# A two-layer hybrid decoder step whose vector, scalar and queue order is set by a scheduler: the scheduler's machine model is exchanged

## The chip, the core and the metric

One core of a Trainium2 chip runs the whole kernel. The metric is the device time of one execution in microseconds; smaller is better. A core has engines with an instruction stream each: PE (TensorE: matmuls, with a loader of its own for the stationary operand, PEld in the profile), DVE (VectorE), ACT (ScalarE), POOL (GpSimd) and SP, which here only issues transfers. An engine runs its stream in order, and an instruction that has to wait for another engine or for a transfer holds back all that stands behind it on the same engine.

## The reference, cut to what matters

512 columns of a prompt and 8 x 4 of a sample group pass through two layers that share all weights (model width 1024, all in float32):

```
h = rmsnorm(x) * (1 + scale1(c)) + shift1(c);   z = h @ W_in
A: causal pooling      B: retention, 4 heads (normed per head, swish gate)
C: short gated conv    D: RWKV-7 time mixing (delta-rule state)
mixed = sum over A..D of sigmoid(gate_n of z) * (branch_n @ W_br_n)
x = x + gate1(c) * (mixed @ W_out)
h2 = rmsnorm(x) * (1 + scale2(c)) + shift2(c)
x = x + gate2(c) * (W_down(silu(a) * b)),   [a|b] = causal_dwconv3(h2 @ W_up)
```

A final rmsnorm follows, and the new states of all mixers are outputs too. The modulation (scales, shifts, gates) is a linear map of silu(c).

## The kernel before

**Tiles.** The 544 columns are handled in two halves of 272. Activations lie with the 1024 features on 128 partitions in 8 blocks. A weight unit is a tile of 128 x 1024, 138 units a layer. `load_unit` (L100 to L112) lets SP load it into `raw` (3 buffers), ACT cast it to a high part `whi` (L110) and DVE subtract to get the low part `wlo` (L111); `whi` and `wlo` have 4 buffers each. Only two units at the start have their subtraction on POOL. Activations are split the same way by `split_hilo`: a cast on ACT (L373), a subtraction on DVE (L374). A product is then three matmuls of 128 x 128 by 272 (`mm3`): high by high (L130), high by low part of the activation (L131), low part of the weight by high (L132). `unit` does this for eight blocks (24 matmuls) into one of three PSUM buffers called `pd`; five more, `pm`, serve the small matmuls.

**Pieces that the prediction speaks of.**
- The start (L890 to L932): x is loaded, its statistic made (L259, L262, L272, L286), the first modulation computed block by block (L196, copied to SBUF by ACT in L198, L201, DVE L203 and L185), x normalised (L926), modulated (L292 to L296) and split (L373, L374), while the first weight units are used block by block.
- RWKV (L377 onward): per pair of heads `p` an inverse norm, made by a sum over partitions (L362), a floor on DVE (L364), Ln on ACT (L365) and Exp on ACT (L370), for two column halves and two pairs. Then DVE forms the scan's operands: L414, L421, L422, and in `products()` L451, L453, L458 from two exponentials (L442, L443). The matmuls L477 and L484 use them. Each different ACT function may need another function table, which an ACT_TABLE_LOAD brings in.
- Then a triangular substitution on DVE: 31 steps of two instructions, L564 and L566, on data that comes back by a transfer (`in_xinit` among them, L537 to L539), and beside it four products L553 that read PSUM of L552. The scan over chunks follows (L583 to L673).
- Retention's norm: L362, then Ln (L367, straight from PSUM) and Exp (L370).
- The gates and branch projections (`gates`, about L1075 to L1117): for each of 8 blocks a `unit` with the gate's weights, whose PSUM goes through a sigmoid on ACT (L1108), and a projection of the branch (6 matmuls a half) whose PSUM is multiplied with it on DVE: L1091 in the first branch, L1093 in the others, which are then added by L1094 (POOL; DVE in the last branch). In the last branch the sum is split (L373, L374) as the operand of W_out, and `residual` (L342 to L348) adds the result to x.
- Short conv: L1022 to L1024, L1047, L1056 to L1065. FFN: L1238 to L1267. The last norm: L308 to L318.

**What sets the order.** The program is emitted in one pass. Small tasks are generators which `slot()` advances after a number of weight matmuls, so that their matmuls lie between the big ones:

```
with tile.TileContext(nc) as tc:
    with tc.manual_schedule(engines={mybir.EngineType.PE}):
        tile_hybrid_step(tc, io)
```

L1538 says that the PE keeps the order in which the program emits its matmuls. For DVE, ACT, POOL and SP the scheduler behind `TileContext` chooses: it plays the program through on a model of the machine and puts instructions in the order in which the model finds them ready. With the order come two other things. Which of a pool's buffers a new tile gets, and so whose end it has to wait for, depends on which tile the model finds free first. And ACT_TABLE_LOADs stand wherever the function on ACT changes in the final order.

## Time and profile before

| | |
|---|---|
| median of 3 runs | 1969.51 us (1968.21 to 1971.51) |
| profiled execution | 1970.54 us, its span 1968.8 us |
| mean granted clock of the PE | 0.997 |
| busy: PE, PEld, DVE, ACT, POOL | 98%, 93%, 53%, 41%, 16% of the span |
| moved | 227.23 MB, 115 GB/s on average |

A row of a timeline reads: start in us, duration in us, engine, line, operation, the tile written, the tiles read, the shape, and how many instructions it takes together; in brackets the idle time of the engine just before it and what ended that. Matmuls overlap: their durations (0.29 us) are longer than their step. The waits group such idle times by the pair of tiles: the line that waited, the line that released it, the total in us, how often, and the longest. Busy time of an engine other than the PE says little here, since it mostly lies beside the PE's.

### The profile page before, as it was taken

The numbers are of one execution on the slowest core, as the hardware profiler recorded it, in microseconds if no ns is written. First come the engines' busy times: TensorE is split into PE (matmuls) and PEld (weight loads), VectorE is DVE, ScalarE is ACT, GpSimd is POOL, SyncE is SP. The second block draws the span as 40 slices with busy tenths as digits, with TensorE's granted clock in tenths as the row PEclk, the third lists the DMA queues.
The fourth block names the chain that finished last, engine by engine and source line by source line (L and its number), as shares of the span: only waits on it lengthen the run. The fifth ranks groups of instructions, "written<-read, shape, count | busy, mean of one in ns | idle before, by whom it ended". The sixth has DMA issues, their size and how long they took to land.

```text
span 1968.8 us, 40136 instructions
## 1 busy us (share of the span) xinstructions
PE 1924.9 (98%) x16868; PEld 1834.8 (93%) x16868; DVE 1046.1 (53%) x2017; ACT 814.8 (41%) x1531; POOL 313.3 (16%) x589
## 2 busy tenths in 40 slices
PE   5999999999999999999999999999999999999997
PEld 5989888899998889999999998889999999999997
DVE  4476443543465444555664765345335665455565
ACT  4642322452355442435445423325423555243541
POOL 1110123213000110112202101241210022011210
PEclk9999999999999999999999999999999999999999
DMA  7324333433346742222332231134224132222221
GB/s 312 98 89 130 116 111 132 161 113 96 122 147 246 305 176 87 89 93 87 119 111 87 64 110 58 63 108 122 82 78 161 52 108 86 86 87 94 89 95 47
DMA packets 75557, 227.23 MB, mean 115 GB/s; under 512 B 20208, under 2 KB 23072, under 8 KB 73584
## 3 DMA queue, kind: packets, MB, share of 16 engines
q1 hardware_dynamic: 69872, 210.43, 32.2%
q0 software_dynamic: 3536, 11.53, 1.7%
q10 hardware_dynamic: 1968, 2.69, 0.5%
q8 instruction: 133, 2.18, 0.4%
q14 instruction: 48, 0.39, 0.1%
HBM read 213.33 MB, written 9.06 MB: 113 GB/s over the span
## 4 chain that ended last, share of the span: by engine, by line
PE 91%; DVE 4%; ACT 2%; DMA 2%; issue 1%; ACTq 0%; POOL 0%; DVEq 0%; POOLq 0%
PE pd L130 28%; PE pd L132 27%; PE pd L131 26%; PE pm L220 2%; DMA raw<-in_wst 1%; ACT whi L110 1%; DVE wlo L111 1%; PE pm L654 1%; PE pm L636 1%; PE pm L605 1%; DMA zr<-zr 1%; PE pm L658 1%; PE pm L593 0%; PE pm L477 0%; PE pm L484 0%
## 5 line engine op out<-in xcount | busy, mean ns | idle before, releaser
L130 PE MATMUL pd<-t,whi 128*128 128x272 f32 x4200 | 1234.8, 294 | 3.2 <-ACT t L373 1.8
L132 PE MATMUL pd<-t,wlo 128*128 128x272 f32 x4200 | 1214.5, 289 | 0.0
L131 PE MATMUL pd<-t,whi 128*128 128x272 f32 x4200 | 1208.5, 288 | 1.0 <-DVE t L374 0.8
L130 PEld LDWEIGHTS pd<-t,whi 128*128 128x128 f32 x4200 | 790.3, 188 | 41.4 <-issue 25.7
L131 PEld LDWEIGHTS pd<-t,whi 128*128 128x128 f32 x4200 | 792.5, 189 | 2.7 <-DVE t L374 1.8
L132 PEld LDWEIGHTS pd<-t,wlo 128*128 128x128 f32 x4200 | 791.3, 188 | 0.0
L111 DVE TENSOR_TENSOR wlo<-raw,whi 128x1024 fp32r<-128x1024 f32 x262 | 324.6, 1239 | 319.6 <-ACT whi L110 319.2
L110 ACT CAST whi<-raw 128x1024 fp32r<-128x1024 f32 x264 | 276.6, 1049 | 429.9 <-PE pd L131 417.3
L1256 POOL COPY off<-zr 128x18 f32<-128x18 f32 x88 | 77.2, 878 | 556.8 <-ACT zr L1254 556.8
L342 DVE SCALAR_TENSOR_TENSOR t<-pd,mod,t 128x272 f32<-128x272 f32 (+1 forms) x160 | 77.0, 482 | 106.9 <-PE pd L132 106.8
L1093 DVE TENSOR_TENSOR zr<-pd,zr 128x272 f32<-128x272 f32 x96 | 41.2, 438 | 124.9 <-PE pd L132 124.7
L1254 ACT COPY zr<-pd 128x272 f32<-128x272 f32 (+2 forms) x264 | 72.7, 311 | 72.9 <-PE pd L132 72.9
L1108 ACT ACTIVATE zr<-pd 128x272 f32<-128x272 f32 x128 | 50.5, 394 | 105.6 <-PE pd L132 105.5
L1094 POOL TENSOR_TENSOR t<-t,zr 128x272 f32<-128x272 f32 x64 | 68.9, 1093 | 119.5 <-DVE zr L1093 119.4
L1023 DVE SCALAR_TENSOR_TENSOR zr<-zr,par,zr 128x560 f32<-128x560 f32 x92 | 73.5, 801 | 9.7 <-ACT zr L1022 9.7
L1022 ACT ACTIVATE zr<-zr,par 128x560 f32<-128x560 f32 x92 | 70.2, 765 | 17.1 <-DVE zr L1047 9.6
L1024 DVE SCALAR_TENSOR_TENSOR zr<-zr,par,zr 128x560 f32<-128x560 f32 x92 | 73.4, 801 | 2.8
L373 ACT CAST t<-zr 128x544 fp32r<-128x544 f32 (+1 forms) x96 | 49.1, 530 | 61.8 <-DVE zr L1267 61.5
L374 DVE TENSOR_TENSOR t<-zr,t 128x544 fp32r<-128x544 f32 (+1 forms) x96 | 54.1, 580 | 30.0 <-ACT t L373 29.0
L259 ACT ACTIVATE zr<-t 128x272 f32<-128x272 f32 (+1 forms) x72 | 32.0, 454 | 86.6 <-DVE t L342 55.9
L610 DVE COPY z<-pm 32x128 f32<-32x128 f32 x34 | 9.8, 289 | 69.7 <-PE pm L605 69.4
L262 DVE TENSOR_TENSOR zr<-zr,zr 128x272 f32<-128x272 f32 (+1 forms) x63 | 29.9, 475 | 20.0 <-ACT zr L259 19.3
(286 smaller groups left out, 1635.1 us busy)
## 6 DMA issues: line engine op xcount, KB each, us to landing
raw<-in_wst SPq DMA_DIRECT2D x276, 512.0 KB, 3.5
t<-in_wada SPq DMA_DIRECT2D x32, 1024.0 KB, 9.7
raw<-in_wada SPq DMA_DIRECT2D x32, 512.0 KB, 3.6
zr<-in_rope POOLq DMA_DIRECT2D x16, 272.0 KB, 3.8
t<-in_xT SPq DMA_DIRECT2D x4, 544.0 KB, 6.7
zr<-zr ACTq DMA_DIRECT2D x32, 68.0 KB, 3.2
t<-in_xT SPq DMA_DIRECT2D x2, 1088.0 KB, 6.8
xs<-t SPq DMA_DIRECT2D x2, 1088.0 KB, 4.6
```

What stands on the lines that cost most here:

```text
L110: S.copy(hi, raw)
L111: (G if (l, u) in ((0, 1), (0, 2)) else V).tensor_tensor(out=lo, in0=raw, in1=hi, op=SUB)
L130: PE.matmul(ps, lhsT=a, rhs=xh, start=first, stop=False)
L131: PE.matmul(ps, lhsT=a, rhs=xl, start=False, stop=False)
L132: PE.matmul(ps, lhsT=b, rhs=xh, start=False, stop=last)
L342: V.scalar_tensor_tensor(out=x[:, c0:c0 + npc], in0=ps[:, :npc], scalar=gate[:, m, 0:1], in1=x[:, c0:c0 + npc], op0=MUL, op1=ADD)
L1022: S.activation(cv, u[:, 0:560], AF.Copy, scale=wcol(0))
L1023: V.scalar_tensor_tensor(out=cv, in0=u[:, 1:561], scalar=wcol(1), in1=cv, op0=MUL, op1=ADD)
L1024: V.scalar_tensor_tensor(out=cv, in0=u[:, 2:562], scalar=wcol(2), in1=cv, op0=MUL, op1=ADD)
L1094: (V if last else G).tensor_tensor(out=a[:, c0:c1], in0=a[:, c0:c1], in1=gs, op=ADD)
L1254: pad_evac(lambda o, i, sl: S.copy(o, i), u, ps, half, 2)
L1256: G.tensor_copy(off[:, 22 * s + j], u[:, 512:562].rearrange("p (x t) -> p x t", t=2)[:, 0:25:3, :])
```

## The change

One argument: the scheduler is to use the timeline simulator as its model of the machine, instead of the one that it has without it.

```diff
-    with tile.TileContext(nc) as tc:
+    with tile.TileContext(nc, schedule_with_timeline_sim=True) as tc:
         with tc.manual_schedule(engines={mybir.EngineType.PE}):
             tile_hybrid_step(tc, io)
```

The computation stays the same, instruction for instruction, and all rows of the PE stay where they are. DVE, ACT, POOL and SP get another order. The rows below group equal neighbours, so their counts differ: 1969 rows on DVE before and 1948 after, with 1208 lines of difference; 1523 and 1535 on ACT, with 653. ACT has six table loads more (42 instead of 36).

**ACT, RWKV's inverse norms in layer 0** (L365 is the Ln, L370 the Exp; `zr_143` belongs to the first pair of heads, `zr_146` to the second; L442 and L443 are the exponentials for the scan's operands). Before:

```order
L365 ACT_TABLE_LOAD
L365 ACTIVATE zr_143_1120<-zr_143_1120,eps_84 128x272 x2
L365 ACTIVATE zr_146_1129<-zr_146_1129,eps_84 128x272 x2
L370 ACT_TABLE_LOAD
L370 ACTIVATE zr_143_1120<-zr_143_1120 128x544
L370 ACTIVATE zr_146_1129<-zr_146_1129 128x544
L442 ACTIVATE zr_157_1179<-pm_156_1176 128x256
L443 ACTIVATE zr_157_1179<-pm_156_1176 128x256
```

After:

```order
L365 ACT_TABLE_LOAD
L365 ACTIVATE zr_143_1120<-zr_143_1120,eps_84 128x272 x2
L365 ACTIVATE zr_146_1129<-zr_146_1129,eps_84 128x272
L370 ACT_TABLE_LOAD
L370 ACTIVATE zr_143_1120<-zr_143_1120 128x544
L365 ACT_TABLE_LOAD
L365 ACTIVATE zr_146_1129<-zr_146_1129,eps_84 128x272
L370 ACT_TABLE_LOAD
L370 ACTIVATE zr_146_1129<-zr_146_1129 128x544
L442 ACTIVATE zr_157_1179<-pm_156_1176 128x256
L443 ACTIVATE zr_157_1179<-pm_156_1176 128x256
```

The last of the four Ln has moved behind the first Exp, and with it two table loads have come in. Layer 1 reads the same.

**DVE, the scan's operands at the same place** (L414 reads the Exp of ACT; L458 writes what the matmul L477 waits for; L1047 belongs to the short conv, L111 is the low part of a weight unit). Before:

```order
L422 TENSOR_TENSOR t4_75_624<-t4_75_624,zr_151_1159 128x544
L421 SCALAR_TENSOR_TENSOR t4_124_1008<-t4_124_1008 128x544
L422 TENSOR_TENSOR t4_75_624<-t4_75_624,zr_152_1163 128x544
L451 TENSOR_TENSOR t4_153_1173<-t4_124_1008,zr_157_1179 64x2x4x31
L453 TENSOR_TENSOR t4_153_1173<-t4_76_625,zr_157_1179 64x2x4x32
L451 TENSOR_TENSOR t4_154_1174<-t4_124_1008,zr_157_1179 64x2x4x31
L453 TENSOR_TENSOR t4_154_1174<-t4_76_625,zr_157_1179 64x2x4x32
L458 TENSOR_TENSOR zr_158_1189<-t4_124_1008,zr_157_1179 128x8x32
L458 TENSOR_TENSOR zr_158_1189<-t4_75_624,zr_157_1179 128x8x32
L1047 TENSOR_TENSOR zr_149_1145<-pd_150_1149,zr_128_1038 128x240
L1047 TENSOR_TENSOR zr_149_1145<-pd_150_1149,zr_128_1038 128x8x4
L111 TENSOR_TENSOR wlo_162_1211<-raw_160_1208,whi_161_1210 128x1024
```

After:

```order
L414 SCALAR_TENSOR_TENSOR t4_124_1008<-t4_75_624,nkk_67_608,zr_146_1129 128x544
L453 TENSOR_TENSOR t4_153_1173<-t4_76_625,zr_157_1179 64x2x4x32
L1047 TENSOR_TENSOR zr_149_1145<-pd_150_1149,zr_128_1038 128x240
L1047 TENSOR_TENSOR zr_149_1145<-pd_150_1149,zr_128_1038 128x8x4
L421 SCALAR_TENSOR_TENSOR t4_124_1008<-t4_124_1008 128x544
L422 TENSOR_TENSOR t4_75_624<-t4_75_624,zr_152_1163 128x544
L451 TENSOR_TENSOR t4_153_1173<-t4_124_1008,zr_157_1179 64x2x4x31
L451 TENSOR_TENSOR t4_154_1174<-t4_124_1008,zr_157_1179 64x2x4x31
L453 TENSOR_TENSOR t4_154_1174<-t4_76_625,zr_157_1179 64x2x4x32
L111 TENSOR_TENSOR wlo_162_1211<-raw_160_1208,whi_161_1210 128x1024
L458 TENSOR_TENSOR zr_158_1189<-t4_124_1008,zr_157_1179 128x8x32
L458 TENSOR_TENSOR zr_158_1189<-t4_75_624,zr_157_1179 128x8x32
```

L1047 and L111 have moved ahead of the two L458, and the second L414 (the first row here) behind the L421 and L422 of the first pair.

**DVE, the start of the substitution in layer 0** (L553 reads the PSUM of L552; the first L564 reads what the transfers bring; `t4_75` is the tile of the substitution). Before:

```order
L558 TENSOR_TENSOR sinv_63_604<-pm_232_1843,cst_82 32x64 x2
L553 TENSOR_TENSOR t4_124_1008<-pm_233_1848,t4_76_625 128x272
L553 TENSOR_TENSOR t4_124_1008<-pm_234_1851,t4_76_625 128x272
L553 TENSOR_TENSOR t4_124_1008<-pm_235_1854,t4_76_625 128x272
L553 TENSOR_TENSOR t4_124_1008<-pm_236_1857,t4_76_625 128x272
L564 TENSOR_TENSOR t4_75_624<-t4_75_624 128x31
L566 TENSOR_TENSOR t4_75_624<-t4_75_624 128x31
L564 TENSOR_TENSOR t4_75_624<-t4_75_624 128x30
```

After:

```order
L558 TENSOR_TENSOR sinv_63_604<-pm_232_1843,cst_82 32x64 x2
L564 TENSOR_TENSOR t4_75_624<-t4_75_624 128x31
L553 TENSOR_TENSOR t4_124_1008<-pm_233_1848,t4_76_625 128x272
L566 TENSOR_TENSOR t4_75_624<-t4_75_624 128x31
L553 TENSOR_TENSOR t4_124_1008<-pm_234_1851,t4_76_625 128x272
L564 TENSOR_TENSOR t4_75_624<-t4_75_624 128x30
L553 TENSOR_TENSOR t4_124_1008<-pm_235_1854,t4_76_625 128x272
L566 TENSOR_TENSOR t4_75_624<-t4_75_624 128x30
L553 TENSOR_TENSOR t4_124_1008<-pm_236_1857,t4_76_625 128x272
L564 TENSOR_TENSOR t4_75_624<-t4_75_624 128x2x29
L566 TENSOR_TENSOR t4_75_624<-t4_75_624 128x2x29
L564 TENSOR_TENSOR t4_75_624<-t4_75_624 128x2x28
```

The four L553 have moved from ahead of the first L564 to places between the substitution's first steps.

**Elsewhere, told in words.** Beside the norm of the second retention (about 432 us) ACT's order before is table load, L367, L367, table load, L1108, table load, L370; after, it is table load, L367, table load, L1108, table load, L367, table load, L370. Ahead of W_out (about 543 us) a pair of L374 stands right behind the last L1093 before; after, three L1094, another L374 and an L111 stand between them (in layer 1 two L111). In the start the copies L198 have moved ahead of weight casts (L110) and of the modulation (L292), and on SP the constants (L928 to L961) and two weight units have moved ahead of the last four pieces of the first modulation's weights (L898). Of the `pd` buffers, 37 gates begin in one whose last reader is an L1091 or L1093, where before it was a sigmoid L1108.

## The prediction

> **What bounds the kernel now.** I read the page's first part, then the waits of the PE alone, then windows and timelines where other engines hold the PE up.
>
> ```profile
> span 1968.8 us, 40136 instructions
> PE 1924.9 (98%) x16868; PEld 1834.8 (93%) x16868; DVE 1046.1 (53%) x2017; ACT 814.8 (41%) x1531; POOL 313.3 (16%) x589
> ```
>
> The PE works for 1924.9 of 1968.8 us, so 43.9 us are all that any order of the other engines could save. The PE's own order is written by hand and the change leaves every row of it alone. So the time changes only where an operand or a free PSUM buffer reaches the PE earlier or later than now. The waits of the PE (line that waits, who released it: us in total, times, longest):
>
> ```profile
> PE pm L272 <- DVE zr L262: 14.9, 2, 13.1
> PE pm L201 <- ACT t L198: 6.6, 2, 5.2
> PE pm L477 <- DVE zr L458: 2.8, 2, 1.4
> PE pm L636 <- DVE z L672: 1.6, 2, 0.8
> PE pd L130 <- DVE zr L346: 1.4, 1, 1.4
> PE pm L362 <- ACT zr L743: 1.2, 1, 1.2
> PE pd L130 <- DVE t L1192: 0.9, 1, 0.9
> PE pm L654 <- DVE z L610: 0.6, 2, 0.3
> ```
>
> The first row is the wait for the first loads (13.1 us) and one wait at the end; nothing there is reordered. Between them little is left to win. A stage without waits gives the price of one weight matmul (columns: window, its length, busy us and count of PE, PEld, DVE, ACT, POOL, clock, DMA share, GB/s):
>
> ```profile
> 800.00:930.00 130.00, 130.00 (x1037) 130.00 (x1037) 75.81 (x115) 60.30 (x109) 24.11 (x53) 1.00 0.28 90
> ```
>
> 130.00 / 1037 = 0.125 us each. The DVE is busy 58% of that window and ACT 46%: enough room for work to move freely, as long as nothing that the PE needs soon is put behind something slow. So I looked in the new order of DVE and ACT for places where a result needed within a few matmuls now stands behind other work. Four such places turned up, each once in each of the two layers.
>
> **First: the scan's operands (L458 to L477), 105 to 117 us.**
>
> ```profile
> 105.20 1.28 ACT L365 ACT_TABLE_LOAD   x1 [2.93 <-DVE zr L364]
> 106.50 1.76 ACT L365 ACTIVATE zr<-zr,eps 128x272 f32<-128x272 f32 x4
> 108.28 1.28 ACT L370 ACT_TABLE_LOAD   x1
> 109.57 1.21 ACT L370 ACTIVATE zr<-zr 128x544 f32<-128x544 f32 x2
> 110.27 1.48 DVE L414 SCALAR_TENSOR_TENSOR t<-t,nkk,zr 128x544 f32<-128x544 f32 x2 [2.58 <-ACT zr L370]
> 111.66 0.72 DVE L421 SCALAR_TENSOR_TENSOR t<-t 128x544 f32<-128x544 f32 x1
> 115.79 0.76 DVE L458 TENSOR_TENSOR zr<-t,zr 128x256 f32<-128x256 f32 x2
> 116.47 0.50 DVE L1047 TENSOR_TENSOR zr<-pd,zr 128x240 f32<-128x240 f32 x2
> 116.89 1.22 DVE L111 TENSOR_TENSOR wlo<-raw,whi 128x1024 fp32r<-128x1024 f32 x1
> 116.61 1.15 PE L477 MATMUL pm<-cst,zr 64*64 64x64 f32 x32 [1.39 <-DVE zr L458]
> ```
>
> Before: four Ln under one table, two Exp under another; the second Exp ends at 109.57 + 1.21 = 110.78. After: Ln, Ln, Ln, table, Exp, table, Ln, table, Exp: two more tables, so from 105.20 on 1.28 + 3 x 0.44 + 1.28 + 0.62 + 1.28 + 0.44 + 1.28 + 0.62, about 113.4. The second L414 waits for that, 2.6 us later. From 110.27 to 116.55 the DVE is dense: 6.28 us of L414 x2, L421 and L422 twice, L451 and L453 twice, L458 x2. After, the first L414, L421 and L422 (0.74 and twice 0.72, each less its overlap with its neighbour: 2.05 us) are done while ACT changes tables, but the two L1047 (0.4 without overlap) and L111 (1.15) have moved ahead of L458: 6.28 - 2.05 + 1.55 = 5.8, from 113.4 on, ends at 119.2 to 119.3. L477 starts about 2.7 to 2.8 us later; I take 2.8, the PE idle there 4.2 instead of 1.39. The waits' row (2.8 us in two) says that layer 1 has the same wait, and its order is the same: 2 x 2.8 = **+5.6**. Bounds: +4 if the DVE packs closer, +7 if L453 must also wait for the Exp behind it.
>
> After a table load the next ACTIVATE starts 0.02 us later (105.20 + 1.28, then 106.50). The Trainium skill ("ScalarE: Activation LUTs", section "What ACT_TABLE_LOAD costs") adds a drain of 1.38 us and has 2.66 us for every switch; by it the two switches would cost 5.3 us a layer and the term would be +11. The rows show no such drain, so the sum goes by 1.28.
>
> **Second: the gate after the substitution (L553, L564, L1091), 162 to 169 us.**
>
> ```profile
> 162.08 1.82 DVE L553 TENSOR_TENSOR t<-pm,t 128x272 f32<-128x272 f32 x4 [0.19 <-PE pm L552]
> 164.07 0.19 DVE L564 TENSOR_TENSOR t<-t 128x31 f32<-128x31 f32 x1 [0.17 <-DMA t<-in_xinit]
> 168.16 0.43 DVE L1091 TENSOR_TENSOR t<-pd,zr 128x272 f32<-128x272 f32 x1
> 168.53 0.37 PE L130 MATMUL pd<-t,whi 128*128 128x272 f32 x1
> ```
>
> Before, the four L553 filled the time until the loads of the substitution landed (164.07). After, the first L564 stands ahead of them and the DVE keeps its order, so all 1.82 us come behind the load. The same sixteen L564 and L566 lie ahead of the first L1091, which ends at about 170.4 instead of 168.59. In the changed kernel the next gate's first matmul takes the PSUM buffer that this L1091 frees (before, one that a sigmoid freed): it starts at about 170.4 instead of 168.53, +1.9, and some 0.1 more at the second half. Two layers: **+4.0**, bounds +2 (half hidden) and +4.5.
>
> **Third: the gate beside the second retention's norm (L367, L1108), 432 to 436 us.**
>
> ```profile
> 432.24 1.28 ACT L367 ACT_TABLE_LOAD   x1
> 433.54 0.87 ACT L367 ACTIVATE zr<-pm,eps 128x272 f32<-128x272 f32 x2
> 434.42 1.28 ACT L1108 ACT_TABLE_LOAD   x1
> 435.71 0.40 ACT L1108 ACTIVATE zr<-pd 128x272 f32<-128x272 f32 x1
> 433.89 0.40 PE L130 MATMUL pd<-t,whi 128*128 128x272 f32 x1 [0.20 <-DVE zr L1093]
> ```
>
> After, the sigmoid L1108 comes between the two L367, with a table load on each side; it ends at 432.24 + 1.28 + 0.44 + 1.28 + 0.40, with the gaps 435.7. That is earlier than now (436.11), but in the changed kernel the matmul of 433.89 gets the buffer which this sigmoid frees, instead of that of L1093. It starts at 435.8: +1.9 a layer, **+3.8**; bounds +2 and +4.6 (a further 0.4 if the next sigmoid is late as well).
>
> **Fourth: the merged branches into w_out (L1094, L374), 542 to 548 us.**
>
> ```profile
> 543.58 0.43 DVE L1093 TENSOR_TENSOR zr<-pd,zr 128x272 f32<-128x272 f32 x1
> 543.93 0.78 DVE L374 TENSOR_TENSOR t<-t,t 128x272 fp32r<-128x272 f32 x2
> 544.99 1.22 DVE L111 TENSOR_TENSOR wlo<-raw,whi 128x1024 fp32r<-128x1024 f32 x1
> 545.55 0.29 PE L131 MATMUL pd<-t,whi 128*128 128x272 f32 x1
> ```
>
> The PE reads the last low part of the first half at 545.55; its L374 ended at 544.71. After, between the L1093 of 543.58 and these two L374 stand three L1094, another L374 and the L111: 0.35 + 4 x 0.35 + 1.14 + 0.78, so 547.2: +1.7. In layer 1 two L111 stand there, one for a w_out tile that lands late; I take 1.8. Sum **+3.5**, bounds +2 and +4.
>
> **The buffers of the gates.** In the changed kernel 37 more gates begin on a buffer that L1091 or L1093 frees, with six matmuls between (0.75 us) instead of a sigmoid with twelve. Such a release is short: the row of 433.89 has 0.20 us where one came late. Between 0 and 18 of them at 0.2: 0 to +3.6; most find the DVE free, so I take **+1.0**.
>
> **What is won.** At the start:
>
> ```profile
> 28.53 1.02 PE L201 MATMUL pm<-cst,t 128*128 128x9 f32 x4 [5.18 <-ACT t L198]
> 27.93 2.25 DVE L374 TENSOR_TENSOR t<-t,t 128x272 fp32r<-128x272 f32 x2 [2.02 <-ACT t L373]
> 27.17 2.35 POOL L111 TENSOR_TENSOR wlo<-raw,whi 128x1024 fp32r<-128x1024 f32 x1 [3.30 <-ACT whi L110]
> 31.35 0.60 PE L130 MATMUL pd<-t,whi 128*128 128x272 f32 x1
> 31.75 0.43 PE L131 MATMUL pd<-t,whi 128*128 128x272 f32 x1
> 35.37 0.32 PE L132 MATMUL pm<-t,wlo 128*128 128x272 f32 x1
> ```
>
> The copy L198 now stands ahead of casts and normalisation, so the 5.18 us go. What is late next is L373 and L374: about 28.3 to 30.2 instead of 31.35, depending on whether the DVE is slowed beside POOL again (L374 took 2.25 us for two beside POOL's L111, 0.78 in the fence above). That wins 1 to 3 us. But constants and weight loads now stand on SP's queue ahead of four pieces of the first modulation weights, and a cast (L110, 1.05 us) ahead of a later L198; that may give it all back. I take **-1.0**, bounds -3 and +3.
>
> Waits that lose their cause in the new order: L346 1.4, L743 1.2, L1192 0.9, L672 1.6, L610 0.6, in sum 5.7. A sigmoid and a statistic stand behind casts elsewhere (about one cast of 1.05, and 0.4 to 0.8 twice). I take **-4.0**, bounds -5.7 and -1.
>
> **Sum.** 5.6 + 4.0 + 3.8 + 3.5 + 1.0 - 1.0 - 4.0 = **+12.9 us**. The profiled execution took 1970.54 us (span 1968.8 and 1.7 around it), so 1983.4; it lies 1.0 above the median of 1969.51, which gives **1982.4**. The half-widths of the seven terms (1.5, 1.25, 1.3, 1, 1.8, 3, 2.4), added as squares, make 5: 1977 to 1988 is the forecast's own range. The runs of before spread over 3.3 us, and about 0.2% (3.9 us) is what a measurement of this kernel can tell from no change.
>
> **Rivals.**
> The PE is slow again after its idle time. A matmul in the start took a step of 3.62 us / 16 = 0.226 (31.75 to 35.37) instead of 0.125, and full speed came 6.8 us after the PE's restart at 28.53. If the 4.2 us idle at L477 throws it back to this pace, up to 6.8 us pass at it, and 1 - 0.125/0.226 = 45% of them are lost: 1.5 to 3 a layer, +3 to +6: 1985 to 1988, with the upper bounds of the terms 1991. For it: the start. Against it: no idle time over 1.4 us occurs in before after the start, so nothing here shows it. Chance 0.15. The Trainium skill ("TensorE: Matmul & The Clock Gate", section "What's actually happening") has a free-running window of 3.4 us, and half the clock after one idle window; by this rule 4.2 us would often, but not always, hold a whole window.
>
> No difference. The PE's order is the same; each delay may fall into slack that I misjudge, and buffers may free in another order than the program's text suggests: 1966 to 1973. Against it: at each of the four places the PE already waits or has under a microsecond to spare. Chance 0.10.
>
> Faster. One mechanism: the order suits the DVE. The first 30 us gain the full 3.0, the named waits go for 5.7, and the second L414 starts early enough that L458 isn't later than now. 1969.5 - 8.7 = 1960.8. It decides as soon as the four places together cost under 8.7 - 3.9 = 4.8 us, a third of what I add up. For it: 6.6 us of waits at L201 show that the present order is poor there. Against it: two more table loads between the Ln and the last Exp delay L414 whatever the DVE's order is. Chance 0.10.
>
> The forecast keeps 0.65. Slower by over 0.2%: 0.65 + 0.15 = 0.80; within 0.2%: 0.10; faster: 0.10. The range goes from 1971 (the sum at the low end with part of the second rival) to 1991.
>
> **What would show it.** In the waits of the changed kernel: L477 on L458 8 us instead of 2.8; L130 on L1091 near 170 and 1148 us and on L1108 near 435 and 1399, 1.9 each; L131 on L374 3.5 instead of 0.8; L201 on L198 down; L346 gone; PE idle about 57 us instead of 44. It is wrong if L477 waits under 2 us each time, or if the start takes the kernel past 31.35 at its first weight matmul; and the first rival holds if matmuls behind L477 step by 0.226 us.

## The result, and the profile after

The changed kernel takes 1984.37 us (median of 4 runs, 1983.78 to 1985.13) beside 1968.86 us (1967.55 to 1971.51) of the kernel before in the same comparison: ratio 1.0077, with a 95% interval of 1.006 to 1.0095. It is slower by 15.5 us; 1982.4 was predicted, within 1971 to 1991. The two profiled executions have spans 14.5 us apart. One execution of the kernel before, in the comparison with e5 to e8, took 7578.43 us; the ratios below leave it out. The page of the changed kernel:

```profile
span 1983.3 us, 40185 instructions
PE 1931.7 (97%) x16868; PEld 1841.3 (93%) x16868; DVE 1043.6 (53%) x2017; ACT 822.6 (41%) x1537; POOL 317.7 (16%) x589
```

The PE has the same 16868 matmul records, yet it is busy for 1931.7 us instead of 1924.9. So the 14.5 us are two things: 7.7 us more idle time (51.6 instead of 43.9) and 6.8 us in which the same matmuls took longer. First the idle time. The waits of the PE, changed kernel:

```profile
PE pm L272 <- DVE zr L262: 15.1, 2, 13.2
PE pm L477 <- DVE zr L458: 8.7, 2, 4.4
PE pd L130 <- ACT t L373: 6.3, 3, 4.8
PE pd L131 <- DVE t L374: 4.6, 4, 1.8
PE pd L130 <- ACT zr L1108: 4.2, 2, 2.1
PE pd L130 <- DVE t L1091: 1.3, 2, 0.7
PE pm L201 <- ACT t L198: 0.5, 1, 0.5
```

All four places are there: L477 (2.8 before), L1091 (none before), L1108 (none before) and L374. Of the four waits in the row of L374 only 0.91 and 1.80 us are the fourth place. The other two, 0.95 us each near 268 and 1249 us, are a fifth that the prediction does not have; in the kernel before they were 0.41 each, which is all of its 0.8. There one L672 stood ahead of this L374 and one behind it (265.94 us); now both stand ahead, and L374 comes 0.5 us later. It is more idle time of 1.1 us in two layers. Both layers read like this:

```profile
267.33 0.70 DVE L672 TENSOR_TENSOR z<-pt,dec 64x128 f32<-64x128 f32 x2
268.05 0.72 DVE L374 TENSOR_TENSOR t<-zr,t 128x544 fp32r<-128x544 f32 x1
```

The waits for L672, L610, L743 and L1192 are gone, that for L346 is down from 1.4 to 0.2. At the start the wait has moved from L198 to L373 (4.8 of the 6.3 us).

Now the slower matmuls. In every one of the traces the granted clock changes only at whole multiples of 3.413 us from its first change, so I show windows of one such step: around L477 in layer 0, around the sigmoid of the second retention, and around L477 in layer 1 (the number after the five engines is the granted clock):

```profile
112.43:115.84 3.41, 0.72 (x7) 0.53 (x5) 3.37 (x9) 1.92 (x4) 3.16 (x8) 1.00 0.01 2
115.84:119.25 3.41, 1.75 (x32) 1.75 (x34) 3.40 (x8) 0.00 (x0) 1.60 (x3) 0.50 0.39 120
119.25:122.67 3.42, 3.42 (x48) 2.49 (x45) 3.23 (x7) 0.59 (x1) 0.00 (x0) 0.50 0.08 34
433.28:436.69 3.41, 1.32 (x11) 1.10 (x10) 1.63 (x3) 3.36 (x5) 1.46 (x2) 1.00 0.37 120
436.69:440.10 3.41, 3.41 (x16) 3.41 (x17) 0.00 (x0) 3.37 (x4) 0.00 (x0) 0.50 0.10 38
1102.29:1105.70 3.41, 0.00 (x0) 0.00 (x0) 3.37 (x8) 0.79 (x3) 3.18 (x8) 1.00 0.00 0
1105.70:1109.11 3.41, 3.04 (x57) 3.05 (x58) 3.38 (x9) 0.59 (x1) 0.36 (x2) 0.50 0.45 154
```

The PE got half its clock for a stretch behind these waits: two steps (6.8 us) at L477 in layer 0, one step (3.4 us) at the sigmoid and at L477 in layer 1. I read the clock in steps of 1 us through both traces from 36 to 1950 us (before that the column shows 1.00 although matmuls step by 0.226, behind it the PE is mostly idle). Each slow stretch is 3.4 or 6.8 us long: one of 3.4 us in the kernel before (near 332 us), and 6.8, 3.4, 3.4, 3.4 and 3.4 in the changed one (near 115, 269, 436, 1105 and 1409), 17 us more. At half clock 17 us lose at most 8.5; 6.8 were lost.

The four places in the changed kernel. L477, timelines of ACT, DVE and PE:

```profile
103.14 1.28 ACT L365 ACT_TABLE_LOAD   x1 [2.95 <-DVE zr L364]
110.90 0.66 ACT L370 ACTIVATE zr<-zr 128x544 f32<-128x544 f32 x1
111.59 0.79 DVE L414 SCALAR_TENSOR_TENSOR t<-t,nkk,zr 128x544 f32<-128x544 f32 x1 [1.62 <-ACT zr L370]
112.64 0.49 DVE L1047 TENSOR_TENSOR zr<-pd,zr 128x240 f32<-128x240 f32 x2
115.56 1.23 DVE L111 TENSOR_TENSOR wlo<-raw,whi 128x1024 fp32r<-128x1024 f32 x1
116.70 0.75 DVE L458 TENSOR_TENSOR zr<-t,zr 128x256 f32<-128x256 f32 x2
117.50 1.97 PE L477 MATMUL pm<-cst,zr 64*64 64x64 f32 x32 [4.36 <-DVE zr L458]
```

From the first table load to the end of L458 it is 14.3 us, where it was 11.35 (105.20 to 116.55): 2.95 more, and the wait is 4.36 instead of 1.39. The 32 matmuls of L477 take 1.97 us instead of 1.15, at half clock. The substitution:

```profile
166.99 0.19 DVE L564 TENSOR_TENSOR t<-t 128x31 f32<-128x31 f32 x1 [1.92 <-DMA t<-in_xinit]
167.09 0.44 DVE L553 TENSOR_TENSOR t<-pm,t 128x272 f32<-128x272 f32 x1
167.44 0.18 DVE L566 TENSOR_TENSOR t<-t 128x31 f32<-128x31 f32 x1
168.79 0.21 DVE L564 TENSOR_TENSOR t<-t 128x58 f32<-128x58 f32 x1
172.45 0.40 PE L130 MATMUL pd<-t,whi 128*128 128x272 f32 x1 [0.59 <-DVE t L1091]
```

The four L553 do come behind the load, but between the steps, and an L553 starts 0.10 us after the step ahead of it, where the next step starts 0.23 after it. The sigmoid and the first matmuls behind it:

```profile
434.27 0.49 ACT L367 ACTIVATE zr<-pm,eps 128x272 f32<-128x272 f32 x1
434.76 1.28 ACT L1108 ACT_TABLE_LOAD   x1
436.06 0.40 ACT L1108 ACTIVATE zr<-pd 128x272 f32<-128x272 f32 x1
436.51 0.46 PE L130 MATMUL pd<-t,whi 128*128 128x272 f32 x1 [2.09 <-ACT zr L1108]
436.76 0.43 PE L131 MATMUL pd<-t,whi 128*128 128x272 f32 x1
439.71 0.43 PE L132 MATMUL pd<-t,wlo 128*128 128x272 f32 x1
```

The gate starts right behind this sigmoid. The matmuls from 436.76 to 439.71 (13 steps in 2.95 us, 0.227 each) are the slow stretch. Ahead of W_out in layer 0:

```profile
545.97 1.13 DVE L1093 TENSOR_TENSOR zr<-pd,zr 128x272 f32<-128x272 f32 x3
548.42 1.22 DVE L111 TENSOR_TENSOR wlo<-raw,whi 128x1024 fp32r<-128x1024 f32 x1
549.56 0.79 DVE L374 TENSOR_TENSOR t<-t,t 128x272 fp32r<-128x272 f32 x2
550.40 0.39 PE L131 MATMUL pd<-t,whi 128*128 128x272 f32 x1 [0.91 <-DVE t L374]
```

The L111 stands between the sums and the pair of L374 that the PE waits for.

### The profile page after: what moved, and what is told of

Its sections match the earlier page's. It is cut to its first block, busy times and chain, and to the rows that moved or that the text cites. A ratio compares the mean times of both kernels' runs of the same rounds, so it can differ in the third digit from the quotient of the medians.

```text
span 1983.3 us, 40185 instructions
## 1 busy us (share of the span) xinstructions
PE 1931.7 (97%) x16868; PEld 1841.3 (93%) x16868; DVE 1043.6 (53%) x2017; ACT 822.6 (41%) x1537; POOL 317.7 (16%) x589
## 4 chain that ended last, share of the span: by engine, by line
PE 92%; DVE 3%; ACT 2%; DMA 1%; issue 1%; SPq 0%; DVEq 0%; ACTq 0%
PE pd L130 28%; PE pd L132 27%; PE pd L131 27%; PE pm L220 2%; PE pm L654 1%; DVE wlo L111 1%; PE pm L605 1%; PE pm L477 1%; PE pm L636 1%; PE pm L658 1%; PE pm L593 0%; PE pm L484 0%; DMA t<-in_xinit 0%; DMA t<-in_xT 0%; PE pm L196 0%
## 5 line engine op out<-in xcount | busy, mean ns | idle before, releaser
L111 DVE TENSOR_TENSOR wlo<-raw,whi 128x1024 fp32r<-128x1024 f32 x262 | 322.4, 1231 | 330.1 <-ACT whi L110 328.8
L110 ACT CAST whi<-raw 128x1024 fp32r<-128x1024 f32 x264 | 276.8, 1048 | 453.2 <-PE pd L131 443.1
L1093 DVE TENSOR_TENSOR zr<-pd,zr 128x272 f32<-128x272 f32 x96 | 40.9, 437 | 124.1 <-PE pd L132 123.7
L1108 ACT ACTIVATE zr<-pd 128x272 f32<-128x272 f32 x128 | 50.5, 394 | 107.7 <-PE pd L132 103.3
L1094 POOL TENSOR_TENSOR t<-t,zr 128x272 f32<-128x272 f32 x64 | 69.2, 1098 | 127.0 <-DVE zr L1093 126.9
L374 DVE TENSOR_TENSOR t<-zr,t 128x544 fp32r<-128x544 f32 (+1 forms) x96 | 54.7, 584 | 29.0 <-ACT t L373 28.8
L373 ACT CAST t<-zr 128x544 fp32r<-128x544 f32 (+1 forms) x96 | 48.5, 531 | 46.7 <-DVE zr L1267 46.3
L610 DVE COPY z<-pm 32x128 f32<-32x128 f32 x34 | 9.8, 289 | 67.3 <-PE pm L605 67.0
```

What stands on the lines that cost most here:

```text
L110: S.copy(hi, raw)
L111: (G if (l, u) in ((0, 1), (0, 2)) else V).tensor_tensor(out=lo, in0=raw, in1=hi, op=SUB)
L1094: (V if last else G).tensor_tensor(out=a[:, c0:c1], in0=a[:, c0:c1], in1=gs, op=ADD)
```

## The experiments

The theory (A): the loss sits at these four places, each once a layer. The waits come from the order and the buffers that the scheduler chose, and the clock falls behind them because of them. Its rivals: the extra table loads, or the order as a whole, are what costs; and the slow matmuls have another cause. All edits but e4's are made in the changed kernel. `tc.issue_after(x)` queues what it holds behind x on x's engine and adds no wait; the other instructions stayed where they were or moved by a few rows, most of all in e7. Equal waits are followed by one slow stretch or by two: 4.36 and 4.35 us in the changed kernel, by 6.8 and 3.4 us. The windows above show why. The first wait leaves the PE idle for 79% of one step of 3.41 us and for 49% of the next, the second for the whole of one step and 11% of the next. The times of most of these kernels scatter by 3.5 to 4.6 us, and the scatter goes with the clock: of the 18 runs of the kernel before beside e9, those with a mean granted clock of 0.998 took 1966.1 to 1968.6 us, those with 0.996 took 1970.0 to 1972.1. So for single places the waits in the trace are the finer measure.

| | median us (runs) | ratio to before, 95% | PE idle us | slow stretches, us in all |
|---|---|---|---|---|
| before (first comparison) | 1968.86 (4) | | 43.9 | 3.4 |
| changed | 1984.37 (4) | 1.0077 (1.006 to 1.0095) | 51.6 | 20.4 |
| e1 | 1984.78 (4) | 1.0067 (1.0052 to 1.0082) | 48.6 | 27.2 |
| e2 | 1978.63 (5) | 1.0038 (1.0025 to 1.0051) | 46.8 | 6.8 |
| e3 | 1985.29 (4) | 1.007 (1.0054 to 1.0087) | 46.7 | 13.6 |
| e4 (in before) | 1976.87 (7) | 1.0039 (1.0028 to 1.005) | 49.0 | 10.2 |
| e5 | 1984.81 (4) | 1.0082 (1.0064 to 1.01) | 50.3 | 23.8 |
| e6 | 1985.78 (4) | 1.0082 (1.0066 to 1.0098) | 52.0 | 20.4 |
| e7 | 1979.00 (4) | 1.0049 (1.0033 to 1.0065) | 47.1 | 20.4 |
| e8 | 1982.80 (4) | 1.0068 (1.0052 to 1.0084) | 47.8 | 23.8 |
| e9 | 1965.61 (11) | 0.9984 (0.9975 to 0.9992) | 38.4 | 6.8 |
| e10 | 1963.75 (8) | 0.997 (0.9959 to 0.998) | 37.2 | 6.8 |

PE idle is span less busy time of the one profiled run of each; the slow stretches are those of the same run, from 36 to 1950 us. The idle time holds the wait for the first loads too, which varies between 12.5 and 13.3 us. The kernel before took 1969.5 (11 runs), 1969.4 (7, the one of 7578.43 among them) and 1969.5 (18) beside e1 to e4, e5 to e8 and e9 with e10.

**e1: the extra table loads taken out.**

```diff
         for p, rs in enumerate(rss):
-            exp_half(rs)
+            with tc.issue_after(ln[0]): exp_half(rs)
```

`ln[0]` is the last of the four Ln.

> The changed kernel, with each Exp (L370) queued behind the last of the four Ln (L365): the two extra table loads a layer go, nothing else of note moves. Theory A (the four places hold the lost time, and at L477 half of the wait is the tables and half the two L1047 and the L111 ahead of L458): the second L414 starts 2.8 us earlier, but L421 and L422 of the first pair (1.3 us) now come after it, so L477's idle time goes from 4.36 to about 2.85 us a layer, -3.0 us in all; if the granted clock then also stays at 1.00 behind L477, another 2.3 us a layer: 1977 to 1981.5. Theory B (the tables lie beside DVE work; only the DVE's order counts): idle stays at 4.4, 1984.

The two Exp, and L477 in layers 0 and 1:

```profile
107.50 1.21 ACT L370 ACTIVATE zr<-zr 128x544 f32<-128x544 f32 x2
116.05 1.88 PE L477 MATMUL pm<-cst,zr 64*64 64x64 f32 x32 [2.91 <-DVE zr L458]
1103.63 1.97 PE L477 MATMUL pm<-cst,zr 64*64 64x64 f32 x32 [2.90 <-DVE zr L458]
```

The waits are 2.9 us, as A said, and theory B falls: the tables were not covered. But the time did not move. The idle time is down by 3.0 us, the busy time up by 3.5 (1935.2): a wait of 2.9 us was still long enough for slow stretches, 3.4 us behind the first and 6.8 behind the second, and others came by elsewhere.

**e2: the L111 behind L458 as well.** e1's edit, and in `load_unit`, where `l458` holds the second L458 once, for the next unit that is loaded:

```diff
-        (G if (l, u) in ((0, 1), (0, 2)) else V).tensor_tensor(out=lo, in0=raw, in1=hi, op=SUB)
+        with tc.issue_after(l458.pop()) if l458 else ExitStack(): (G if (l, u) in ((0, 1), (0, 2)) else V).tensor_tensor(out=lo, in0=raw, in1=hi, op=SUB)
```

> As e1, and the one L111 that stands ahead of the two L458 queued behind them (1.13 us). Theory A: L477's idle time about 1.7 us a layer, clock at 1.00 behind it, so 2 x (2.65 + 2.3) = 9.9 us off: 1974.5. If the slow matmuls behind L477 (1.97 us for 32 instead of 1.15) come from something other than the idle time, they stay, and 1979 comes out. Theory B: only 1.1 us a layer less, 1982.

L477 in both layers:

```profile
115.44 1.15 PE L477 MATMUL pm<-cst,zr 64*64 64x64 f32 x32 [1.78 <-DVE zr L458]
1097.54 1.15 PE L477 MATMUL pm<-cst,zr 64*64 64x64 f32 x32 [1.77 <-DVE zr L458]
```

The wait is 1.78 us, and now the 32 matmuls take 1.15 us again: no slow stretch at either L477. The span is 9.8 us shorter than the changed kernel's, but the profiled run is the fastest of the five, and it also lacks the slow stretch near 268 us, which the edit does not touch. The medians are 5.7 apart: 1978.63 was measured, 1974.5 forecast.

**e3: the PE kept busy while it waits.**

```diff
-            psB = PM()
+            psB = PM(); [PE.matmul(psB[:, 0:256], lhsT=ident, rhs=cst[:, 0:256], start=True, stop=True) for _ in range(9 if T == 0 else 0)]
```

> The changed kernel with nine extra matmuls of 128x128 by 256 (into the PSUM tile that L477 overwrites) just ahead of the first L477 in each layer. They compute nothing that is used. They fill most of the 4.36 us in which the PE waits. Theory A1 (the granted clock falls because the PE idles there): the wait for L458 ends at the same time, the L477, L484, L220 and weight matmuls behind it run at full pace, 2.3 us a layer less: 1979.8. Theory A2 (the clock falls for another reason, or the slow pace belongs to these small matmuls): no gain, 1984 or more.

L477 in both layers, and between them a wait that is new:

```profile
118.28 1.15 PE L477 MATMUL pm<-cst,zr 64*64 64x64 f32 x32 [0.48 <-DVE zr L458]
317.49 0.39 PE L130 MATMUL pd<-t,whi 128*128 128x272 f32 x1 [1.43 <-ACT zr L1108]
1109.31 1.15 PE L477 MATMUL pm<-cst,zr 64*64 64x64 f32 x32 [0.47 <-DVE zr L458]
```

L458 comes as late as ever, but the matmuls behind it run at full pace in both layers (1.15 us), so A1 holds at this place: from L477 to the next group of L437 the kernel is 2.3 us faster than the changed one (its lag goes from +0.8 to -1.5). The total did not fall. Near 317 us a wait of 1.43 us for a sigmoid queued behind a cast (L110) came in that the changed kernel did not have there, with a slow stretch right behind it (319.15 to 322.56). Another came near 340 us, behind a step in which the PE was not idle. Together they took 5 us back. Why a shift of some tenths of a us made that sigmoid late was not settled.

**e4: the table loads put into the kernel before.**

```diff
-            exp_half(rs)
+            x = exp_half(rs); p or tc.add_manual_dep(ln[0], x.name, mybir.DependencyInfo(mybir.DependencyClass.NoSync, mybir.DependencyReason.DATA), reason="order")
```

The dependency queues the fourth Ln behind the first Exp on ACT.

> The kernel before, with only the fourth Ln (L365) queued behind the first Exp (L370), which brings the two extra table loads a layer of the changed kernel and leaves L1047 and L111 behind L458. Theory A: the second L414 starts 2.8 us later, 1.3 us of it are filled by L421 and L453, L477's idle time goes from 1.39 to about 2.9 us: +3.0 us for both layers; with a fall of the clock behind it up to +4.6 more: 1972 to 1976.5. Theory B: no change, 1969.

L477 in both layers:

```profile
117.95 1.42 PE L477 MATMUL pm<-cst,zr 64*64 64x64 f32 x32 [3.81 <-DVE zr L458]
1103.04 1.97 PE L477 MATMUL pm<-cst,zr 64*64 64x64 f32 x32 [3.80 <-DVE zr L458]
```

The tables alone are enough to make the kernel before slower, by 7.4 us. The wait is 3.8 us where I had 2.9: an exponential (L442) also slipped ahead of the second Exp, and the DVE found less to do meanwhile. So the tables alone add 2.4 us a wait, and the DVE's order alone (e1) 1.5, but both together 2.97. In the changed kernel the DVE does an L421 and an L422 (108.61 to 109.97 us) while ACT changes tables; in e4 these two came only after the late L442, and the DVE stood idle for 2.75 us there.

**e5: the four L553 ahead of the substitution again.**

```diff
         for s in range(31):
-            substitute(s)
+            with tc.issue_after(l553): substitute(s)
```

> The changed kernel, with the substitution's first instruction (L564) queued behind the last of the four L553, as it stands in the kernel before. Theory A (the L553 behind the load cost what the trace of the changed kernel shows: the PE waits 0.59 and 0.69 us for L1091): both waits go, 1.3 us less, 1983. Theory B (the prediction's size, 2.0 us a layer, part of it hidden in something else): 4 us less, 1980.5.

The waits for L1091 (1.28 us) are gone from the trace, and 0.21 us for an L1093 near 1516 us is all that came in: theory A. The median (1984.81) does not show it; 1.1 us is within the scatter.

**e6: one table load less at the sigmoid, same buffer.**

```diff
-        ln_bones(sq, TOK, 1.0 / 64, EPS6, rs)
+        ln_bones(sq, TOK, 1.0 / 64, EPS6, rs); M["ln"] = ln[-1]
...
-                    S.activation(gs, ps[:, :HALF], AF.Sigmoid)
+                    with tc.issue_after(M.pop("ln")) if "ln" in M else ExitStack(): S.activation(gs, ps[:, :HALF], AF.Sigmoid)
```

> The changed kernel, with the sigmoid (L1108) beside each retention's norm queued behind the second Ln (L367): the second retention has one table load less a layer, ACT's order there is that of the kernel before, but the gate still begins in the PSUM buffer that this sigmoid frees. Theory A (the wait comes from that buffer): the sigmoid ends 0.45 us later, the PE waits 2.5 instead of 2.1 us in each layer, 0.9 us more: 1985. Theory B (the extra table load is what costs): 1.3 us a layer less and no fall of the clock behind it, 1979 to 1982.

The gate's first matmul in both layers:

```profile
437.23 0.39 PE L130 MATMUL pd<-t,whi 128*128 128x272 f32 x1 [2.48 <-ACT zr L1108]
1409.41 0.39 PE L130 MATMUL pd<-t,whi 128*128 128x272 f32 x1 [2.49 <-ACT zr L1108]
```

The wait grew by 0.39 us although a table load of 1.28 went and ACT's order there became that of the kernel before. So at this place it is not the number of table loads: the wait follows the end of the sigmoid whose buffer the gate begins in. A gate in its old buffer was not tried.

**e7: the sigmoid ahead of the two Ln.**

```diff
-        ln_bones(sq, TOK, 1.0 / 64, EPS6, rs)
+        pss = [(PM(), c0, c1) for c0, c1 in HS]; [PE.matmul(ps[:, :HALF], lhsT=bones, rhs=sq[:, c0:c1], start=True, stop=True) for ps, c0, c1 in pss]
+        if p: yield -14
+        with tc.issue_after(sgm[0]) if p else ExitStack(): [S.activation(rs[:, c0:c1], ps[:, :HALF], AF.Ln, bias=EPS6, scale=1.0 / 64) for ps, c0, c1 in pss]
```

`sgm[0]` is the last sigmoid emitted; L1108 becomes L1109 in this kernel.

> The changed kernel, with the two Ln (L367) of the second retention emitted 14 weight matmuls later and queued behind the sigmoid (L1108), which then needs no table load of its own and runs as soon as its matmuls end. Theory A: the PE's wait there falls from 2.1 to about 0.4 us a layer; with it goes the slow stretch of 3.4 us behind it, which costs about 1.6: 2 x (1.7 + 1.6) = 6.6 us less, 1978. If the slow stretch has another cause it stays, 1981. Theory B (the wait moves on to the retention's result, which comes 0.5 us later): 1983 or more.

What waits for a sigmoid near this place in either layer:

```profile
440.29 0.39 PE L130 MATMUL pd<-t,whi 128*128 128x272 f32 x1 [0.15 <-ACT zr L1109]
1411.57 0.39 PE L130 MATMUL pd<-t,whi 128*128 128x272 f32 x1 [0.17 <-ACT zr L1109]
```

The windows behind the place in layer 0, the granted clock after the five engines:

```profile
436.00:440.00 4.00, 4.00 (x33) 3.92 (x32) 2.17 (x3) 2.42 (x4) 0.00 (x0) 1.00 0.04 14
440.00:444.00 4.00, 3.85 (x31) 3.71 (x30) 2.14 (x3) 1.47 (x3) 1.55 (x2) 1.00 0.10 14
```

What is left are 0.15 and 0.17 us at a later gate, and the clock stays at 1.00. Both slow stretches behind the sigmoid are gone; two others came by near 1245 and 1309 us, so the sum of slow stretches is unchanged (20.4 us), and the idle time fell by 4.5 us where 3.4 was forecast. The median is 5.4 us lower (1979.0; 1978 forecast), close to theory A, though not by its two terms.

**e8: the weights' low parts behind L374.** With `load_unit` as in e2, and `split_hilo` handing back its L374:

```diff
-                        split_hilo(a[:, c0:c1], mix[m // 4][:, m % 4, c0:c1], mix[2 + m // 4][:, m % 4, c0:c1])
+                        lo = split_hilo(a[:, c0:c1], mix[m // 4][:, m % 4, c0:c1], mix[2 + m // 4][:, m % 4, c0:c1]); l458[:] = [lo] * 3 if (m, half) == (7, 0) else l458
```

> The changed kernel, with the next three L111 of each layer queued behind the L374 of the last first half ahead of W_out. Theory A: the waits of L131 for L374 there (0.91 and 1.80 us) go, 2.7 us less, 1981.7. Theory B (the L111 are late then, and the PE waits for a low part of weights instead): 1984 or more, with a wait of L132 for L111 in the trace.

The waits of 0.91 and 1.80 us are gone, no wait for L111 has come in their place, and those for L1091 are 0.5 us shorter in sum. The median is 1.6 us lower, where 2.7 was forecast; both are within the scatter.

**e9 and e10: all four mended, and then the start.** e9 has the edits of e2, e5, e7 and e8; e10 also:

```diff
-        (G if (l, u) in ((0, 1), (0, 2)) else V).tensor_tensor(out=lo, in0=raw, in1=hi, op=SUB)
+        V.tensor_tensor(out=lo, in0=raw, in1=hi, op=SUB)
```

> The changed kernel with the edits of e2, e5, e7 and e8 together: all four places mended, everything else (the start, the gates' buffers, the small gains) as the change made it. Theory A (these places hold the loss): the PE idles 5.2 us less at L477, 1.3 at L1091, 3.9 at the sigmoid and 2.7 at L374, so about 38.5 us in all (51.6 in the changed kernel, 43.9 in the one before); and the slow stretches behind them go, 1.2 to 1.7 us each: 1962 to 1966, below the kernel before. Theory B (the loss is spread over the order, and mending moves the waits on): above 1970.

> As e9, with the low parts (L111) of the weight units 1 and 2 of layer 0 on DVE instead of POOL. In the changed kernel POOL's two L111 take 5.68 us and one DVE instruction of 128x9 beside them (L185) 2.30 instead of 0.17. If that is what holds L292 and so the first weight matmul, the DVE does three L111 of 1.22 in turn, L185 ends about 0.8 us earlier and the first weight matmul starts at 28.2 to 29.2 instead of 29.9: 0.7 to 1.7 us below e9. If the loads set that time, no difference.

The busy times of e9, from its page:

```profile
PE 1925.3 (98%) x16868; PEld 1836.6 (94%) x16868; DVE 1045.8 (53%) x2017; ACT 812.1 (41%) x1529; POOL 319.7 (16%) x589
```

The start on DVE in the changed kernel, beside POOL's two subtractions:

```profile
25.08 2.30 DVE L185 SCALAR_TENSOR_TENSOR scl<-mod,par 128x9 f32<-128x9 f32 x1
```

The same instruction in e10:

```profile
26.16 0.16 DVE L185 SCALAR_TENSOR_TENSOR scl<-mod,par 128x9 f32<-128x9 f32 x1
```

The idle time of e9 is 38.4 us (38.5 forecast) and its busy time is back at 1925.3, 0.4 above the kernel before. With 1965.61 us it is below both kernels. Mending the four places takes 19.6 us off the span, where the change had put on 14.5; with them mended, the rest of the new order is worth 3.9 us. The fifth place is still in e9 (0.95 us twice, with a slow stretch near 264 us behind the first). In e10 the DVE does the two subtractions itself, L185 takes 0.16 us instead of 2.30, and the first weight matmul starts at 28.14 instead of 29.91 (29.51 in e9): 1963.75 us, 1.9 below e9 where 0.7 to 1.7 was forecast, 0.3% below the kernel before, the best of all that were run.

## Why the prediction was right, and where its steps were off

The direction, the places and the range were right. The sum came out near the truth partly by chance: its terms are all waits, and the waits grew by 7.7 us, not by 12.9; the other 6.8 us are the first rival, which had a chance of 0.15. Term by term (predicted, and measured as the change of idle time in the two traces):

| | predicted us | measured us |
|---|---|---|
| L477 | +5.6 | +5.9 (4.36 and 4.35 for 1.39 twice) |
| the gate after the substitution | +4.0 | +1.3 (0.59, 0.69) |
| the gate beside the retention's norm | +3.8 | +3.8 (2.09, 2.11 for 0.20, 0.21) |
| L374 ahead of W_out | +3.5 | +2.7 (0.91, 1.80) |
| the buffers of the gates | +1.0 | 0 |
| the start | -1.0 | -1.3 (0.49 + 4.85 for 1.44 + 5.18) |
| waits that go, less small losses | -4.0 | -4.7 (the rest of the 7.7; in it +1.1 of the fifth place) |
| the PE's clock | 0 (a rival: +3 to +6) | +6.8 |

**L477.** Right in size. Its parts were taken as a plain chain; e1 and e4 show that the tables and the DVE's order overlap (2.4 and 1.5 alone, 2.97 together).

**The substitution.** This is the step that failed most: "all 1.82 us come behind the load". They do, but they do not add up. Four instructions of the substitution alone took 0.90 us (164.07 to 164.97); the same four with four L553 between took 1.80 (166.99 to 168.79). An L553 fits into the gap that each of them leaves before the next can start. The cost on the DVE is 0.90 us, and since the load also lands earlier against the PE (2.9 us later than before, where the PE is 3.3 behind), 0.6 to 0.7 us reached the PE.

**The retention's norm.** Right, and by the mechanism named as far as it was tested: e6 and e7 show that the wait follows the sigmoid's end, not the table load beside it.

**L374.** The prediction let the chain begin at the last L1093 at 543.58, where the kernel before has it. The chain has the length that was said (3.7 us), but it begins earlier: the last of the three L1093 that follow each other from 545.97 starts at 546.67, by the PE's lag of 3.9 us that is 542.7 in the old time. That is the 0.8 us missing in layer 0; layer 1 came as said.

**The gates' buffers.** No such gate waits for an L1093 in the changed kernel.

**The clock.** The prediction lets the time change only where an operand or a free buffer reaches the PE earlier or later. This step left something out: 6.8 of the 14.5 us are matmuls that took longer. It had the slower matmuls as a rival, but at L477 only, at 4.2 us of idle time, with an argument against it that no longer wait existed in the trace. The trace of the kernel before already held one slow stretch, near 332 us, which the prediction's windows pass by. A wait of 4.2 us holds a whole step of 3.41 us in (4.2 - 3.41) / 3.41 = 23% of its positions, not "often" as the prediction has it. Half clock came at L477 all the same (6.8 and 3.4 us slow), and also at the sigmoid, behind 2.1 us, and near 268, behind the fifth place. e2 and e3 show the cause at L477: with the wait shortened, or filled with matmuls that nobody needs, the same L477 run at 1.15 us. The price of a wait here is thus its length and, if it fills enough of a step, some 1.4 us for each slow stretch (6.8 us for the 17 more, in portions of 3.4).

**The range.** The sum came within 3 us because the two errors, 5 us too much of waiting and 7 us too little for the clock, have opposite signs: that is luck. The range was wide enough for either error alone (about 1977 or 1989).

## What to carry to other kernels

A scheduler's choice on the engines that are not the bound is read by the few results which the bound engine needs within the next dozen instructions: look for a table switch, an unrelated long instruction, or a buffer whose last reader is late, and price the place by its rows. Where the PE is near 100% busy, a wait of 2 us can cost more than itself, because the clock can fall behind it; mending four such places made a slower kernel the faster one. Between small dependent instructions on DVE, independent work costs less than its duration.

## What the runs showed of the hardware

The clock fell after less idle time than I expected, and in fixed portions. Between 36 and 1950 us all slow stretches are 3.4 us or twice that, and they begin and end on steps of 3.413 us that lie differently against the start of the program in every trace (the first change of the clock is at 33.92 us in the changed kernel and at 35.43 in the one before). What tells best is the PE's idle share of one step. I counted the steps that run at full clock in all twelve traces, from the first change to 1950 us. Of those with the PE idle for over 60% of the step all 24 were followed by half clock; of those with 40 to 60%, 17 of 29; below 40% only six of more than 6600. In each of these six the PE was never idle, but the step held the 64 matmuls of L685, with 8 columns each; the stretch near 332 us in the kernel before is one of them:

```profile
329.55 2.04 PE L685 MATMUL pm<-t,zr 64*64 64x8 f32 x64
```

So the length of a wait alone does not tell. The clock stayed behind 1.39 us (before), 1.80 us (the changed kernel, 41% of a step) and even 2.09 us (the sigmoid of layer 0 in e3, 52%); it fell behind 1.43 us in e3 (near 317 us, 46% of a step together with a short wait) and behind 2.1 us at the sigmoid both times in the changed kernel (61 and 62%). Near 268 us two waits of 0.71 and 0.95 us close together were followed by a slow stretch in the changed kernel (49%) and in e1, e3 and e5 to e10, but not in e2 (31%), where a step ends inside the second wait. The Trainium skill ("TensorE: Matmul & The Clock Gate", section "What's actually happening") has the free-running window of 3.4 us, and the length of the stretches and their steps agree with it; it wants a whole idle window, and there the measurement differs: 2.1 us of idle time with busy time on both sides were enough. What decides between 40 and 60% was not measured.

A switch of ACT's tables cost 1.28 us in every trace, with the next instruction 0.01 to 0.02 us later where its operand was there; two of them delayed the second Exp in layer 0 by 2.85 us (its end is 108.71 in e1 and 111.56 in the changed kernel). A DVE instruction on 128x9 elements took 2.30 us beside two subtractions of 128x1024 on POOL and ended with them (27.38 and 27.36 us), and 0.16 without them.
